# Where the taps of a convolution and the pieces of an output projection stand in the order of a two-layer hybrid trunk

## The chip, the core and the metric

The kernel runs on one core of one Trainium2 chip. The metric is the device time of one execution in microseconds; the time given for a kernel is the median of its runs. Traces come from one profiled execution. Engines are named as in the profile: PE is TensorE, DVE VectorE, ACT ScalarE, POOL GpSimd, SP SyncE.

## What is computed

Two decoder layers over 512 tokens of width 1024, in float32. Of each layer the part that matters here is its first half:

```python
n = rmsnorm(h, mix_norm[i])
u = n @ w_in[i]                                   # 1024 -> 9 x 256 columns
a_val, a_gate, pool_in, q, k, v, gb, gc, sv = jnp.split(u, IN_SPLITS, axis=-1)
y_a = conformer_conv(a_val, a_gate, ...)          # glu, causal depthwise conv of 31 taps, layernorm, silu
y_b = pool_mixer(pool_in, ...)                    # causal window means of 2, 4, 8, 16
y_c = diff_attention(q, k, v, ...)                # 4 heads x 2 maps, rotary, softmax(a0) - lam * softmax(a1)
y_d = short_gated_conv(gb, gc, sv, ...)           # 3 taps
h = h + jnp.concatenate([y_a, y_b, y_c, y_d], -1) @ w_out[i]
```

After it come a mixture of sixteen experts (top 2 of one group of four), a gated embedding projection, and at the end of the second layer a norm.

## The kernel before

Matrix products that must be exact to float32 are done as three products of split operands: each value is a high part and a low part (`wh`/`wl` for weights, `nhi`/`nlo`, `mhi`/`mlo` for activations), and `mm3` (L255 to L257) multiplies high by high, high by low and low by high. ScalarE makes the high half of a weight tile (L228), VectorE the low half (L239); `w.get` makes them three half units ahead of their use, and SP's queue loads the raw tiles four units ahead.

*The projection* (`project`, L431) goes through units of 256 columns; a half unit is 24 matmuls of 512 columns. After each half unit `tick` (L157) is called with a budget, `BUDGET`, less the cost of other VectorE work of that half unit. It first issues what is due, then takes entries from a queue while any budget is left:

```python
for c, fn in self.due.pop(self.t, []):
    fn()
    budget -= c
while self.queue and budget > 0:
    c, fn = self.queue.pop(0)
    fn()
    budget -= c
```

In the queue stand the 31 taps of the long convolution for each of two halves of the channels, 62 a layer, each an instruction on VectorE over 512 tokens (L480 for the first, L483 for the others), entered at a cost of 0.6; behind them stands the layer norm (`layer_norm`, L646). That is a cost in the planner's own units, not a time. GpSimd sums the pooling windows meanwhile (L513).

*Attention* (`attend`, L693) has 16 steps, one for a head and a block of 128 queries, and each engine's work of one step follows the list `TICK` (L53): transposes of q and k (L721), row maxima of the step before (L770), additions of finished pieces to the residual h (L750), attention times values (L816), exponentials (L784), the piece `f1`, the transpose of the combined probabilities (L804, copied by ScalarE at L806), what is due, the scores (L762), the piece `f2`, the combination of the two maps (L795 to L797). `due` goes on with the queue of taps, with budgets of its own (`TAPS`, L54); when the taps are used up, layer norm enters it and spreads its stages over the next steps: transposes (L656), statistics (L658, L661), a reciprocal root on GpSimd (L204, L205), normalising (L666), transposes back (L671), scale and tanh on ScalarE (L673, L675), the product (L678), and the split into `mhi` (L682) and `mlo` (L686).

The output projection of a block of 128 tokens, a half of its columns and a half of its rows is two *pieces*, each of six matmuls (L255 to L257 with `mhi`, `mlo`). The first 16 pieces read the pooling and short convolution outputs and can run from the start; three are issued before the first step, thirteen are dealt out by the tables `FILL1` (the piece or pieces at `f1` of step n) and `FILL2` (at `f2`). The others need layer norm and attention and start at step 11 (`WO1`); an entry that asks for more pieces than there are gets what is left:

```python
while k > 0 and (cur or (fill and fill[0][0] <= n)):
    ...
"f1": lambda n: filler(2 * n, FILL1[n]),
"f2": lambda n: filler(2 * n + 1, FILL2[n]),
```

A piece pair accumulates in one PSUM bank and keeps it until its addition to h. In attention eight banks are split into four for scores and pieces, three for transposes, one for the attention output.

Of the kernel before, what the change touches and what calls it, by code (L numbers as in the profile page):

```python
# [40 lines left out]
NCON, NCON2, NCON3 = 322, 256, 512  # L41
NOIDX = 2048.0
PAD_L, PAD_R, PAD_M = 224, 224, 160
BUDGET = 3.1
NRING, NRING2, NRING3, NRING4 = 4, 3, 4, 2
WO1 = 22
FILL1 = [0, 1, 1, 1, 1, 1, 0, 5, 1, 1, 1, 1, 1, 4, 0, 1, 0, 2, 1, 1, 0, 0, 0, 0, 0, 0, 0, 0, 0]
FILL2 = [4, 0, 1, 0, 0, 1, 0, 4, 1, 0, 0, 1, 0, 0, 0, 1, 2, 1, 2, 1, 2, 2, 4, 2, 2, 2, 0, 0, 0]
WARM0, WARM, PRE = 17, 11, 7
TAILU, POST, FIRST, FIRST4 = 9, 3, 5, 1  # L50
HI = {5: 1, 6: 2, 9: 3, 10: 4}
# [116 lines left out]
class _Kernel:  # L168
# [255 lines left out]
    def cm_unit(self, between=None, cost=0.0):  # L424
        o = [self.mm([128, S]) for _ in range(2)]
        for hf in range(2):
            self.cm_half(o, self.w.get(between=between if hf == 0 else None), hf)
            self.ticks.tick(BUDGET - cost if hf == 0 else BUDGET)
        return o

    def project(self):  # L431
# [154 lines left out]
        for hf in range(2):  # L586
            hi, lo = (t.rearrange("p (c n) -> p c n", c=4) for t in w.get(between=ev_gb if hf == 0 else None))
            for i in range(NT):
                ts = slice(i * 128, (i + 1) * 128)
                for c in range(4):  # L590
                    k = 4 * hf + c
                    self.mm3(o_v[i], self.nhi[:, k, ts], self.nlo[:, k, ts], hi[:, c], lo[:, c], k == 0, k == 7)
            tk.tick(BUDGET - (2.4 if hf == 0 else 0))
        pb_.close_()
# [10 lines left out]
        def qk(i, half, k0):  # L605
            ts = slice(i * 128, (i + 1) * 128)
            hi, lo = (t.rearrange("p (c n) -> p c n", c=2) for t in half)
            for c in range(2):
                k = k0 + c
                self.mm3(o[i], self.nhi[:, k, ts], self.nlo[:, k, ts], hi[:, c], lo[:, c], k == 0, k == 7)  # L610
# [3 lines left out]
        for hf in range(2):  # L614
            if hf:
                half = w.get()
            for i in range(NT):
                qk(i, half, 2 * hf)
            tk.tick(BUDGET)
        hv = [w.get(1), w.get(1)]  # L620
# [72 lines left out]
    def attend(self):  # L693
# [201 lines left out]
        def filler(n, k):  # L895

            while k > 0 and (cur or (fill and fill[0][0] <= n)):
                if not cur:
                    a = fill.pop(0)[1]
                    cur.append((a, wo_mm(*a)))  # L900
                    next(cur[0][1])
                else:
                    (i, nh, kh), g = cur.pop()
                    next(g)
                    if (nh, kh) == (1, 1) and i < 2:
                        for d, f in zip(FND, (fn1, fn3, fn2, fn4, fn5)):
                            tk.later(d, lambda f=f, i=i: f(i))
                k -= 1
# [35 lines left out]
        def each(table, f):  # L944
# [20 lines left out]
            "hi": lambda n: n in HI and w.make_hi(base + HI[n]),  # L965
            "f1": lambda n: filler(2 * n, FILL1[n]),
            "f2": lambda n: filler(2 * n + 1, FILL2[n]),
        }
# [608 lines left out]
```

## Time and profile before

| | |
|---|---|
| median of 3 runs | 923.5 us (921.14 to 924.35) |
| profiled execution | 922.49 us, span 920.7 us |
| projection, first layer | about 20 to 122 us of the span |
| attention steps, first layer | 130 to 200 us |
| projection, second layer | about 470 to 571 us |
| attention steps, second layer | 580 to 650 us |

The span is what lies between the first and the last instruction of the trace; 1.8 us of the execution lie around it. In a row of the timeline the first number is the start in us from the span's start, the second the length of the run of instructions that the row merges (their count is at its end), and in square brackets stands how long the engine was idle before and what it waited for. An instruction's length in the trace overlaps the next one's start a little, so a run of n is shorter than n times the mean length.

### The profile page before, as it was taken

Reading aid. Unit: us, or ns where it says so; the run is one execution under the profiler, and the core shown is the slowest. Engines: PE = TensorE matmul, PEld = TensorE weight load, DVE = VectorE, ACT = ScalarE, POOL = GpSimd, SP = SyncE. Lnnn points to the kernel's source line nnn. Section 1 sums busy time; section 2 is a strip of 40 time slices with the busy share of each in tenths; the row PEclk is TensorE's granted clock in tenths of the full one; section 3 lists DMA queues with packets and bytes.
Section 4 is the critical chain, followed back from the end, with each engine's and each line's share of the span. In section 5 each row is a group of like instructions: output and inputs, shape, how many; then the busy total and the mean of one; then the engine's idle time right before and its main releaser. Section 6 shows DMA issues by size and latency. Waiting matters only on the chain. (4 is left out here: it accounts for less than half of the span.)

```text
span 920.7 us, 12343 instructions
## 1 busy us (share of the span) xinstructions
PE 852.5 (93%) x4393; PEld 684.7 (74%) x4393; DVE 707.4 (77%) x1182; ACT 515.4 (56%) x929; POOL 155.2 (17%) x214
## 2 busy tenths in 40 slices
PE   6999999897999999989979999989969999998894
PEld 5888877785677777667878887767847777776783
DVE  4499979966788888746676987998478888885674
ACT  4322236853687877745433232487437778776453
POOL 2050001122222211101010400022131222111101
PEclk8999999998999999999999999999979999999998
DMA  9322330158799979663322233110968998882602
GB/s 346 116 92 92 103 114 1 47 195 308 266 347 363 370 272 340 236 221 160 115 92 92 92 103 115 46 47 29 386 219 296 373 370 311 315 320 94 258 24 91
DMA packets 35775, 179.02 MB, mean 194 GB/s; under 512 B 8064, under 2 KB 8320, under 8 KB 18944
## 3 DMA queue, kind: packets, MB, share of 16 engines
q1 hardware_dynamic: 23472, 148.49, 43.1%
q0 software_dynamic: 9792, 20.99, 6.2%
q10 hardware_dynamic: 2448, 8.73, 2.7%
q8 instruction: 35, 0.57, 0.3%
q14 instruction: 28, 0.23, 0.1%
HBM read 171.89 MB, written 23.07 MB: 212 GB/s over the span
## 5 line engine op out<-in xcount | busy, mean ns | idle before, releaser
L239 DVE TENSOR_TENSOR wl<-wr,wh 128x1024 fp32r<-128x1024 f32 x212 | 255.1, 1230 | 44.4 <-ACT wh L228 43.2
L228 ACT CAST wh<-wr 128x1024 fp32r<-128x1024 f32 x212 | 216.2, 1053 | 92.6 <-PE mm L256 61.0
L255 PE MATMUL mm<-wh,xTh 128*128 128x512 f32 x256 | 114.5, 447 | 0.7 <-ACT xTh L221 0.7
L257 PE MATMUL mm<-wh,xTl 128*128 128x512 f32 x256 | 101.3, 396 | 1.2 <-DVE xTl L222 1.2
L256 PE MATMUL mm<-wl,xTh 128*128 128x512 f32 x256 | 100.8, 394 | 0.0
L483 DVE SCALAR_TENSOR_TENSOR acc<-glu,cwh,acc 128x512 f32<-128x512 f32 x120 | 90.5, 819 | 0.1
L257 PE MATMUL mm<-nhi,wl 128*128 128x512 f32 (+1 forms) x224 | 77.3, 345 | 2.5 <-DVE wl L239 2.5
L255 PE MATMUL mm<-nhi,wh 128*128 128x512 f32 (+1 forms) x224 | 77.1, 344 | 0.0
L256 PE MATMUL mm<-nlo,wh 128*128 128x512 f32 (+1 forms) x224 | 77.0, 344 | 0.0
L255 PEld LDWEIGHTS mm<-wh,xTh 128*128 128x128 f32 x256 | 48.4, 189 | 16.6 <-issue 6.7
L1198 POOL DMA_INDIRECT xg<-xnd,ix x32 | 34.9, 1091 | 151.1 <-PE tr L251 137.9
L1241 PE MATMUL mm<-wr,hT 128*128 128x512 f32 x128 | 60.2, 592 | 0.0
L256 PEld LDWEIGHTS mm<-wl,xTh 128*128 128x128 f32 x256 | 48.5, 190 | 15.4 <-DVE wl L239 6.2
L257 PEld LDWEIGHTS mm<-wh,xTl 128*128 128x128 f32 x256 | 48.2, 188 | 12.8 <-DVE xTl L222 2.7
L255 PE MATMUL mm<-wh,mhi 128*128 128x512 f32 x128 | 54.1, 422 | 0.4 <-DVE h L750 0.4
L1203 POOL DMA_INDIRECT yd<-ys,ix x32 | 32.3, 1011 | 122.9 <-ACT ys L1243 107.3
L255 PE MATMUL mm<-wh,n3h 128*128 128x512 f32 x128 | 50.5, 395 | 0.0
L257 PE MATMUL mm<-wh,mlo 128*128 128x512 f32 x128 | 50.3, 393 | 0.0
L256 PE MATMUL mm<-wl,mhi 128*128 128x512 f32 x128 | 50.0, 390 | 0.0
L257 PE MATMUL mm<-wh,n3l 128*128 128x512 f32 x128 | 49.9, 390 | 0.0
L256 PE MATMUL mm<-wl,n3h 128*128 128x512 f32 x128 | 49.9, 390 | 0.0
L221 ACT CAST xTh<-tr 128x512 fp32r<-128x512 f32 x64 | 34.5, 590 | 25.2 <-PE tr L251 23.7
(235 smaller groups left out, 1860.6 us busy)
## 6 DMA issues: line engine op xcount, KB each, us to landing
wr<-wgu SPq DMA_DIRECT2D x62, 1024.0 KB, 9.2
wr<-wdn SPq DMA_DIRECT2D x30, 1024.0 KB, 11.0
wr<-win SPq DMA_DIRECT2D x13, 1024.0 KB, 6.6
wr<-wout SPq DMA_DIRECT2D x8, 1024.0 KB, 4.8
wr<-wpg SPq DMA_DIRECT2D x8, 1024.0 KB, 14.2
yt<-yd SPq DMA_DIRECT2D x12, 512.0 KB, 8.5
wr<-wqk SPq DMA_DIRECT2D x4, 1024.0 KB, 4.7
xnd<-xn ACTq DMA_DIRECT2D x8, 512.0 KB, 6.5
```

Source lines behind the costliest of these rows:

```text
L221: self.SC.copy(hi, src)
L228: self.SC.copy(hi, src)
L239: self.V.tensor_sub(lo, src, h32)
L255: self.T.matmul(o, lh, rh, start=first, stop=False)
L256: self.T.matmul(o, lh, rl, start=False, stop=False)
L257: self.T.matmul(o, ll, rh, start=False, stop=last)
L483: V.scalar_tensor_tensor(acc[:, m], glu[:, m, k:k + S], self.cwh[:, m, k:k + 1], acc[:, m], op0=ALU.mult, op1=ALU.add)
L1198: return self.G.indirect_dma_start(out=dst, out_offset=None, in_=self.xnd[:, :], in_offset=bass.IndirectOffsetOnAxis(ap=col, axis=0), boun ...
L1203: return self.G.indirect_dma_start(out=self.yd[:, :], out_offset=bass.IndirectOffsetOnAxis(ap=col, axis=0), in_=src, in_offset=None, bound ...
L1241: self.T.matmul(o[nh], hT[:, c], wc[:, ns], start=(c == 0), stop=(c == 1))
```

## The change

The budget of a half unit in the projection goes from 3.1 to 3.7, and the two tables deal the thirteen pieces out differently: of before there were four at `f2` of step 0 and up to five asked for at `f1` of step 7 (two were left); now two stand at `f2` of step 0, and one at `f1` of each step up to step 9.

```diff
-BUDGET = 3.1
+BUDGET = 3.7
-FILL1 = [0, 1, 1, 1, 1, 1, 0, 5, 1, 1, 1, 1, 1, 4, 0, 1, 0, 2, 1, 1, 0, 0, 0, 0, 0, 0, 0, 0, 0]
-FILL2 = [4, 0, 1, 0, 0, 1, 0, 4, 1, 0, 0, 1, 0, 0, 0, 1, 2, 1, 2, 1, 2, 2, 4, 2, 2, 2, 0, 0, 0]
+FILL1 = [0, 1, 1, 1, 1, 1, 1, 1, 1, 1, 1, 1, 1, 4, 0, 1, 0, 2, 1, 1, 0, 0, 0, 0, 0, 0, 0, 0, 0]
+FILL2 = [2, 0, 1, 0, 0, 1, 0, 0, 0, 0, 0, 1, 0, 0, 0, 1, 2, 1, 2, 1, 2, 2, 4, 2, 2, 2, 0, 0, 0]
```

The instructions of SP's queue stay in the same order. On VectorE the taps in the projection change as follows (`acc<-glu,cwh,acc` is a tap, `wl<-wr,wh` the low half of a weight tile), from the first half units of the first layer; first before:

```order
L480 TENSOR_SCALAR acc<-glu,cwh,par 128x512 x2
L483 SCALAR_TENSOR_TENSOR acc<-glu,cwh,acc 128x512 x2
L239 TENSOR_TENSOR wl<-wr,wh 128x1024
L483 SCALAR_TENSOR_TENSOR acc<-glu,cwh,acc 128x512 x6
L239 TENSOR_TENSOR wl<-wr,wh 128x1024
L483 SCALAR_TENSOR_TENSOR acc<-glu,cwh,acc 128x512 x6
L239 TENSOR_TENSOR wl<-wr,wh 128x1024
```

And the same place now:

```order
L480 TENSOR_SCALAR acc<-glu,cwh,par 128x512 x2
L483 SCALAR_TENSOR_TENSOR acc<-glu,cwh,acc 128x512 x3
L239 TENSOR_TENSOR wl<-wr,wh 128x1024
L483 SCALAR_TENSOR_TENSOR acc<-glu,cwh,acc 128x512 x7
L239 TENSOR_TENSOR wl<-wr,wh 128x1024
L483 SCALAR_TENSOR_TENSOR acc<-glu,cwh,acc 128x512 x7
L239 TENSOR_TENSOR wl<-wr,wh 128x1024
```

One tap more stands in every half unit that has any; a layer has eleven such places, so 61 taps stand in the projection and not 50.

VectorE in the second and third step of the first layer's attention (`mx` row maxima, `h` an addition of a finished piece, `fac` and `e` the combination of the two maps), before:

```order
L770 TENSOR_REDUCE mx<-mm 128x1 x2
L750 TENSOR_TENSOR h_113<-h_113,mm 128x512
L750 TENSOR_TENSOR h_114<-h_114,mm 128x512
L713 TENSOR_TENSOR qks<-qr_968,qks 128x8x32
L483 SCALAR_TENSOR_TENSOR acc<-glu,cwh,acc 128x512 x4
L795 RECIPROCAL fac<-sums 128x1
L796 SCALAR_TENSOR_TENSOR fac<-fac,nlam,sums 128x1
L797 SCALAR_TENSOR_TENSOR e_1274<-e_1276,fac,e_1274 128x128
L770 TENSOR_REDUCE mx<-mm 128x1 x2
L750 TENSOR_TENSOR h_115<-h_115,mm 128x512
L483 SCALAR_TENSOR_TENSOR acc<-glu,cwh,acc 128x512 x4
```

And now (`bst`, `bmv` are layer norm's statistics):

```order
L770 TENSOR_REDUCE mx<-mm 128x1 x2
L750 TENSOR_TENSOR h_113<-h_113,mm 128x512
L713 TENSOR_TENSOR qks<-qr_977,qks 128x8x32
L658 BN_STATS bst<-tr 128x6
L661 BN_AGGR bmv<-bst 128x2
L795 RECIPROCAL fac<-sums 128x1
L796 SCALAR_TENSOR_TENSOR fac<-fac,nlam,sums 128x1
L797 SCALAR_TENSOR_TENSOR e_1268<-e_1270,fac,e_1268 128x128
L770 TENSOR_REDUCE mx<-mm 128x1 x2
L750 TENSOR_TENSOR h_114<-h_114,mm 128x512
L666 TENSOR_SCALAR acc<-acc,bmv,lr 128x2x128
```

The eight taps are gone from these steps, one addition has moved a step down, and layer norm begins in the second step, three steps sooner.

TensorE in the ninth step of the first layer's attention, up to its scores (`tr<-con,qks` transposes of q or k, `oacc` attention times values, `tr<-con,e` the transpose of the probabilities, `tr<-con,acc` those of layer norm), before:

```order
L721 MATMUL tr<-con,qks 96x128 x4
L816 MATMUL oacc<-v_961,at 128x64
L816 MATMUL oacc<-v_962,at 128x64
L804 MATMUL tr<-con,e_1582 128x128 x2
L671 MATMUL tr<-con,acc 128x128 x2
L656 MATMUL tr<-con,acc 128x128 x2
L845 MATMUL tr<-con,on 128x128 x2
L762 MATMUL mm<-KT,QT 128x384
```

And now:

```order
L816 MATMUL oacc<-v_970,at 128x64
L816 MATMUL oacc<-v_971,at 128x64
L255 MATMUL mm<-wh,mhi 128x512
L256 MATMUL mm<-wl,mhi 128x512
L257 MATMUL mm<-wh,mlo 128x512
L255 MATMUL mm<-wh,mhi 128x512
L256 MATMUL mm<-wl,mhi 128x512
L257 MATMUL mm<-wh,mlo 128x512
L804 MATMUL tr<-con,e_1609 128x128 x2
L845 MATMUL tr<-con,on 128x128 x2
L762 MATMUL mm<-KT,QT 128x384
```

A piece stands now between the attention output and the transpose, and layer norm's transposes have gone to earlier steps.

## Rows read from the trace of the kernel before

**Rows 1.** The page, busy us of the engines.

```profile
PE 852.5 (93%) x4393; PEld 684.7 (74%) x4393; DVE 707.4 (77%) x1182; ACT 515.4 (56%) x929; POOL 155.2 (17%) x214
```

**Rows 2.** Busy time by stage: stretch and length, engines, granted clock, DMA share, GB/s.

```profile
500.00:570.00 70.00, 70.00 (x352) 59.29 (x351) 63.93 (x92) 19.51 (x27) 12.84 (x12) 1.00 0.24 82
...
579.60:626.00 46.40, 40.42 (x242) 31.84 (x240) 43.96 (x120) 32.59 (x95) 7.59 (x14) 1.00 0.13 46
590.00:600.00 10.00, 9.53 (x59) 7.65 (x58) 9.35 (x30) 5.73 (x20) 0.62 (x2) 1.00 0.01 2
611.00:626.00 15.00, 11.26 (x81) 8.81 (x78) 13.70 (x36) 14.51 (x42) 3.07 (x5) 1.00 0.21 71
```

**Rows 3.** VectorE's timeline in the second layer's projection, up to attention.

```profile
498.94 1.23 DVE L239 TENSOR_TENSOR wl<-wr,wh 128x1024 fp32r<-128x1024 f32 x1 [1.12 <-ACT wh L228]
...
504.38 1.23 DVE L239 TENSOR_TENSOR wl<-wr,wh 128x1024 fp32r<-128x1024 f32 x1 [0.24 <-ACT wh L228]
505.52 6.49 DVE L483 SCALAR_TENSOR_TENSOR acc<-glu,cwh,acc 128x512 f32<-128x512 f32 x6
...
513.94 5.90 DVE L483 SCALAR_TENSOR_TENSOR acc<-glu,cwh,acc 128x512 f32<-128x512 f32 x6
...
538.54 0.69 DVE L222 TENSOR_TENSOR mlo<-sA,mhi 128x512 fp32r<-128x512 f32 x1 [1.21 <-ACT mhi L221]
539.87 0.69 DVE L222 TENSOR_TENSOR mlo<-sA,mhi 128x512 fp32r<-128x512 f32 x1 [0.64 <-ACT mhi L221]
...
560.22 4.07 DVE L483 SCALAR_TENSOR_TENSOR acc<-glu,cwh,acc 128x512 f32<-128x512 f32 x6
...
572.36 0.94 DVE L713 TENSOR_TENSOR qks<-qr,qks 128x256 fp32r<-128x256 f32 x2 [4.44 <-ACT qks L708]
```

**Rows 4.** GpSimd's timeline there: the first and the last of six window sums.

```profile
504.91 1.62 POOL L513 TENSOR_TENSOR sA<-up 128x527 f32<-128x527 f32 x1 [30.27 <-ACT up L504]
...
507.08 1.58 POOL L513 TENSOR_TENSOR sB<-sA 64x526 f32<-64x526 f32 x1
...
516.16 1.81 POOL L513 TENSOR_TENSOR sB<-sA 64x520 f32<-64x520 f32 x1
```

**Rows 5.** TensorE's timeline at the entry into the second layer's attention.

```profile
572.85 1.96 PE L721 MATMUL tr<-con,qks 128*96 128x128 f32 x16 [1.71 <-DVE qks L713]
```

**Rows 6.** What TensorE waited for, 579.6 to 626: us, times, longest.

```profile
PE oacc L816 <- ACT at L806: 2.0, 2, 1.3
PE tr L721 <- ACT at L806: 1.0, 1, 1.0
PE tr L804 <- DVE e L797: 0.8, 4, 0.3
PE tr L845 <- ACT at L806: 0.7, 1, 0.7
PE mm L762 <- ACT e L784: 0.6, 2, 0.3
```

**Rows 7.** What ScalarE waited for, 579.6 to 626.

```profile
ACT e L784 <- DVE mx L770: 3.5, 3, 1.4
```

**Rows 8.** TensorE's timeline: the first scores, one of two pieces, the eighth, ninth, twelfth scores.

```profile
579.68 0.36 PE L762 MATMUL mm<-KT,QT 96*128 96x256 f32 x1
...
608.27 0.48 PE L255 MATMUL mm<-wh,mhi 128*128 128x512 f32 x1
...
611.09 0.38 PE L804 MATMUL tr<-con,e 128*128 128x128 f32 x2
...
611.44 0.36 PE L762 MATMUL mm<-KT,QT 96*128 96x256 f32 x1
...
615.75 0.42 PE L762 MATMUL mm<-KT,QT 96*128 96x384 f32 x1
...
625.85 0.42 PE L762 MATMUL mm<-KT,QT 96*128 96x384 f32 x1
```

**Rows 9.** VectorE's timeline: the first of three groups of taps in attention.

```profile
579.75 2.73 DVE L483 SCALAR_TENSOR_TENSOR acc<-glu,cwh,acc 128x512 f32<-128x512 f32 x4
```

## The prediction

> **What bounds the kernel now.** I read the page's first section, then busy time by stage, then VectorE's timeline through the second layer's projection and attention, then who waits for whom in attention. Over the span TensorE is busy 93% and VectorE 77% [rows 1], but that average hides two different stages. In the projection TensorE is busy 70.00 of 70.00 us while VectorE has 63.93 [rows 2]: TensorE alone sets the time there, and nothing it waits for is late. From the first scores of attention to the twelfth (the 46.4 us of the second row of that group) TensorE is busy 40.42, so it stands idle 5.98, and VectorE is busy 43.96, the fuller of the two. The third and fourth rows split this: from 590 to 600 TensorE idles 0.47 in 10 us; from 611 to 626 it idles 3.74 in 15, VectorE has 13.70 and ScalarE 14.51. So the early steps are packed with projection pieces on TensorE and the late ones wait. For whom is in [rows 6]: the largest rows name ScalarE's copy of the turned probabilities (L806), 2.0, 1.0 and 0.7 us; only 0.8 names VectorE. But ScalarE itself waited 3.5 us for VectorE's row maxima (L770) [rows 7], so part of what is booked on ScalarE comes from a late VectorE. The first layer shows the same steps; all numbers below are from the second, whose clock was 1.00 in these rows.
>
> **The change, part by part.** Two things move, nothing is added: of the 62 taps of a layer 50 ran in the projection and 12 in attention (three groups of four); now 61 and 1 do. And of the thirteen pieces of the output projection that run up to the tenth step, two leave the stretch after the first scores and one the stretch after the seventh; one each goes to the stretches after the sixth, eighth and ninth.
>
> *Taps in the projection.* A tap costs 4.07/6 = 0.68 us (the row at 560.22 of [rows 3]). I follow VectorE's lateness through its waits. The first extra tap falls before a wait of 1.12 us and vanishes in it. The second meets 0.24: 0.44 late. Five more come before the next wait: 0.44 + 5 x 0.68 = 3.84 late. There two waits of 1.21 and 0.64 for ScalarE give 1.85 back: 1.99 late. The last four: 4.71 late at the end of the taps. Then VectorE sits idle 4.44 us before the first L713 (the row at 572.36 of [rows 3]), so 0.27 is left, and since TensorE waits for just that instruction with 1.71 us already [rows 5], I charge 0.3 us a layer. Before that point nothing shows: VectorE makes the low halves of the weights (L239) three half units before TensorE reads them, and one half unit is 504.38 - 498.94 = 5.44 us, so 4.7 us late is under the 16.3 of the cover. The loads on SP's queue that wait for these halves keep their order and stand four units ahead. If the 4.44 us were not there, all 4.71 would fall on TensorE.
>
> What is least sure is the tap's price where GpSimd works. From 504.91 to 517.97 its window sums run [rows 4], and the two groups of six taps in that stretch took 6.49 and 5.90 us, up to 1.08 each instead of 0.68 (the rows at 505.52 and 513.94 of [rows 3]). VectorE has no gap there already, so an extra tap does not lengthen GpSimd's work: it is pushed behind it, and I price it at 0.68. The other end is 1.08 for every one of the eleven: 11.9 us, less the cover of 0.68 + 0.24 + 1.85 + 4.44 = 7.21, is 4.7 us late a layer. There is no end below nothing: the instructions only grow in number.
>
> That the two engines are in each other's way is also in the Trainium skill (SBUF — State Buffer, "Who interferes with whom"): a VectorE instruction with two inputs in SBUF and a GpSimd one that reads SBUF exclude each other for the whole instruction. By that rule a tap could wait for a whole sum of 1.58 us [rows 4]; for the three extra taps of that stretch that is 4.7 us more, about the far end just given and a slower kernel. The trace agrees that they collide, not with that size: 0.40 us a tap.
>
> *Attention.* Taken out of VectorE: 11 x 0.68 = 7.5 us of 43.96, leaving 36.5; TensorE's work stays 40.4. Two bounds follow. If every wait of TensorE goes, a layer gains 5.98; if the softmax chain and not VectorE's load is what it waits for, nothing (or what [rows 6] books on VectorE, 0.8). A gain above 5.98 is excluded, since TensorE has no less to do; a loss here needs a new wait, see below. The pieces move at no cost of their own: one is (611.09 - 608.27)/2 = 1.41 us [rows 8], the stretch from 611.44 to 615.75 has no piece today and holds waits, and what the others gain the first and seventh give back.
>
> For the middle I use the two rows of [rows 2]. Up to 611 the stretch is 46.4 - 15 = 31.4 us with 5.98 - 3.74 = 2.24 us of waits. With one piece a step and VectorE at 93% the row from 590 to 600 idles 0.047 of its time, so 1.5 us stay. From 611 on there were no taps to take away (the last of the three groups of four that begin at 579.75 [rows 9] ends before 593) and VectorE is still busy 13.70 of 15 us, so what helps there is indirect: layer norm starts three steps earlier, so its VectorE and ScalarE work leaves this stretch, and pieces fill waits. I let half of the 3.74 stay, 1.9. So 1.5 + 1.9 = 3.4 stay and 2.6 us a layer go. What layer norm moves with it (transposes, ScalarE copies and activations, two short GpSimd instructions a block) lands in steps 1 to 5, where ScalarE has 5.73 of 10 us and GpSimd 0.62 [rows 2].
>
> New waits: a piece that is split over two steps keeps one of four PSUM banks while the next scores need two, so scores can wait for the exponentials that free the last pair. Today that is 0.6 us in two waits, 0.3 each [rows 6]. Bounds: nothing, or 0.3 in each of five steps, 1.5; I count it inside the 3.4 that stay.
>
> *Sum.* (2.6 - 0.3) x 2 layers = 4.6 us. The profiled execution took 922.49, span 920.7 and 1.8 around it: 922.49 - 4.6 = 917.9. The median shown, 923.5, is 1.0 above the profiled one: **918.9**.
>
> **Rivals.**
> *All waits go* (for it: work sums put TensorE alone on top, 40.4 against 36.5; against: the late stretch had no taps and still idles). (5.98 - 0.3) x 2 = 11.4: 912.1.
> *The chain sets the steps, not the load.* Scores, maxima, exponentials, combination, transpose, copy follow one another across engines; for it: the large rows of [rows 6] name ScalarE, which is busy 14.51 of 15 in that stretch. Then only the 0.8 booked on VectorE goes: (0.8 - 0.3) x 2 = 1.0: 922.5, no change.
> *VectorE enters attention late.* Place: the first L713 after the projection. Price: the far end of the taps, 4.7 us a layer, for it the 1.08 us of the taps beside GpSimd, against it that most extra taps run where GpSimd is idle. It makes the kernel slower from the point at which L713 comes more than 2.6 us later than now; at 4.7: (4.7 - 2.6) x 2 = 4.2 more: 927.7.
> That the change would not do what it says is excluded for the counts by the order of the instructions.
>
> **How the numbers follow.** About 0.3%, 2.8 us, is what a measurement of this kernel can tell from no change, so faster means under 920.7 and slower above 926.3. Forecast 0.52 (its own range 915 to 921), all waits 0.06, chain 0.28, late VectorE 0.14. Faster: 0.49 of the forecast, 0.06, and 0.05 of the chain case, where a little more goes: 0.60. Same: the remaining 0.03 and 0.23: 0.26. Slower 0.14. The range from 914 to 925 leaves out the all-waits case and the late VectorE, 0.20.
>
> **What would show it.** After: a tap group of one and not of four at the first step; VectorE's wait before the first L713 of attention shrunk from 4.44 to under 0.5 us, TensorE's wait there 1.7 to 2.2; no wait of TensorE in the projection; twelfth scores 2.6 us sooner after the first ones; TensorE's waits in that stretch 3.4 us and not 6. Wrong if L713 is over 1 us late, if the waits of [rows 6] on L806 stay whole (chain), or if attention gains and the mixture of experts behind it does not start as much earlier.

## The result, and the profile after

The changed kernel takes 911.65 us (median of 7 runs, 910.83 to 916.55) where the kernel before, beside it, took 922.54 (919.62 to 924.35): ratio 0.9895, 95% interval 0.9873 to 0.9917. The profiled execution took 910.88, its span 909.1, against 922.49 and 920.7. So the change is worth about 11 us where 4.6 were forecast: the sign was right, the size was not, and the time lies under the range.

The page of after, busy us of the engines ([rows 1]). TensorE's instructions are as many and its total is nearly what it was, so the 11.6 us of span are not work that went away:

```profile
PE 851.7 (94%) x4393; PEld 684.5 (75%) x4393; DVE 706.6 (78%) x1182; ACT 515.0 (57%) x929; POOL 157.6 (17%) x214
```

Busy time by stage in the second layer of after ([rows 2]; the same stages, 5.5 us sooner at the first scores): the projection, attention from the first scores to the twelfth, and from that stretch its early and its late part. Columns are stretch, length, PE, PEld, DVE, ACT, POOL, granted clock, DMA share, GB/s:

```profile
495.00:565.00 70.00, 70.00 (x352) 59.27 (x351) 68.12 (x99) 19.54 (x27) 13.12 (x12) 1.00 0.23 79
574.10:615.60 41.50, 39.24 (x243) 31.86 (x240) 37.18 (x111) 32.89 (x96) 8.24 (x14) 1.00 0.15 52
584.50:594.50 10.00, 9.68 (x61) 7.68 (x60) 9.44 (x33) 8.57 (x29) 0.95 (x2) 1.00 0.01 2
600.60:615.60 15.00, 13.70 (x90) 11.01 (x88) 14.10 (x36) 13.10 (x37) 2.96 (x4) 1.00 0.20 71
```

TensorE is still busy 70.00 of 70.00 us in the projection, though VectorE now has 68.12. Attention is where the time went: from the start of the first scores to that of the twelfth it is 615.58 - 574.20 = 41.38 us, against 46.17 in [rows 8], and 41.38 against 46.21 in the first layer. That is 9.6 of the 11.6 us. The last 15 us of the stretch idle 1.30 and not 3.74. The remaining 2 us are not put down to the change: the first scores of the two layers come 0.3 us sooner each, 0.4 gather between the twelfth scores of the second layer and the experts behind it, and 0.9 come at the head of these experts, behind a wait for a DMA. There the granted clock was 0.60 in the 4.3 us from the first transposes (L251) on in before, and 1.00 in after; the transposes, before and after:

```profile
682.70 1.77 PE L251 MATMUL tr<-con,xg 128*128 128x128 f32 x8 [1.91 <-DMA xg<-xnd,ix]
672.06 1.09 PE L251 MATMUL tr<-con,xg 128*128 128x128 f32 x8 [1.71 <-DMA xg<-xnd,ix]
```

VectorE's timeline of after in the projection and at the door of attention (its first transposes), seven taps to a group ([rows 3]):

```profile
500.37 7.96 DVE L483 SCALAR_TENSOR_TENSOR acc<-glu,cwh,acc 128x512 f32<-128x512 f32 x7
508.25 1.21 DVE L239 TENSOR_TENSOR wl<-wr,wh 128x1024 fp32r<-128x1024 f32 x1
509.39 6.57 DVE L483 SCALAR_TENSOR_TENSOR acc<-glu,cwh,acc 128x512 f32<-128x512 f32 x7
515.88 1.22 DVE L239 TENSOR_TENSOR wl<-wr,wh 128x1024 fp32r<-128x1024 f32 x1
...
566.87 0.94 DVE L713 TENSOR_TENSOR qks<-qr,qks 128x256 fp32r<-128x256 f32 x2 [0.21 <-ACT qks L708]
```

And TensorE's of after: the door ([rows 5]), the first and the twelfth scores ([rows 8]):

```profile
567.36 1.95 PE L721 MATMUL tr<-con,qks 128*96 128x128 f32 x16 [1.71 <-DVE qks L713]
...
574.20 0.36 PE L762 MATMUL mm<-KT,QT 96*128 96x256 f32 x1
...
615.58 0.42 PE L762 MATMUL mm<-KT,QT 96*128 96x384 f32 x1
```

VectorE's 4.44 us of idle time ahead of L713 are down to 0.21, and TensorE waits there the same 1.71 as before. What TensorE waits for in attention, 574.1 to 615.7 (us in total, times, longest; [rows 6]):

```profile
PE mm L762 <- DVE h L750: 0.7, 1, 0.7
PE mm L762 <- ACT e L784: 0.6, 1, 0.6
PE tr L804 <- DVE e L797: 0.4, 2, 0.2
PE tr L721 <- DVE qks L713: 0.4, 1, 0.4
PE oacc L816 <- ACT at L806: 0.3, 1, 0.3
```

The waits for the copy L806, 3.7 us in three rows before, are one of 0.3. The fourth row lies ahead of the first scores. ScalarE's wait for the row maxima in the same stretch ([rows 7]) has halved:

```profile
ACT e L784 <- DVE mx L770: 1.8, 4, 0.9
```

### The profile page after: what moved, and what is told of

Read it like the earlier page. It is cut to its first block, busy times and chain, and to the rows that moved or that the text cites. A ratio compares the mean times of both kernels' runs of the same rounds, so it can differ in the third digit from the quotient of the medians.

```text
span 909.1 us, 12343 instructions
## 1 busy us (share of the span) xinstructions
PE 851.7 (94%) x4393; PEld 684.5 (75%) x4393; DVE 706.6 (78%) x1182; ACT 515.0 (57%) x929; POOL 157.6 (17%) x214
## 5 line engine op out<-in xcount | busy, mean ns | idle before, releaser
L239 DVE TENSOR_TENSOR wl<-wr,wh 128x1024 fp32r<-128x1024 f32 x212 | 253.2, 1221 | 42.0 <-ACT wh L228 40.5
L483 DVE SCALAR_TENSOR_TENSOR acc<-glu,cwh,acc 128x512 f32<-128x512 f32 x120 | 91.7, 830 | 0.1
L257 PEld LDWEIGHTS mm<-nhi,wl 128*128 128x128 f32 x224 | 42.4, 189 | 8.1 <-DVE wl L239 3.2
```

The lines of the kernel that those rows point to most:

```text
L239: self.V.tensor_sub(lo, src, h32)
L257: self.T.matmul(o, ll, rh, start=False, stop=last)
L483: V.scalar_tensor_tensor(acc[:, m], glu[:, m, k:k + S], self.cwh[:, m, k:k + 1], acc[:, m], op0=ALU.mult, op1=ALU.add)
```

## The experiments

All ratios are to the kernel before on the same chip, with 95% intervals. To compare steps, the start of the first matmul of each step's scores (L762) is taken from TensorE's timeline and the differences are summed: "early" is first to sixth scores, "late" sixth to twelfth. The stretch holds the same 14 pieces in every kernel; the old tables put 10 into the early part and 4 into the late one, the new tables 8 and 6.

| kernel | taps in attention | tables | layer norm | early | late | sum |
|---|---|---|---|---|---|---|
| before | 12 | old | late | 22.40 | 23.77 | 46.17 |
| no_att_taps | 0 | old | late | 20.81 | 23.84 | 44.65 |
| budget_only | 1 | old | early | 21.87 | 22.44 | 44.31 |
| tables_only | 12 | new | late | 21.79 | 24.60 | 46.39 |
| late_norm | 1 | new | late | 18.09 | 24.59 | 42.68 |
| after | 1 | new | early | 19.15 | 22.23 | 41.38 |

(budget_only and tables_only from the first layer, whose granted clock was 1.00 over the whole stretch; the others from the second, at 1.00 too.)

### One half of the change at a time: budget_only and tables_only

```diff
-BUDGET = 3.1
+BUDGET = 3.7
```

> Only the taps move (budget 3.7), the pieces stand as before. The span from the first to the twelfth scores of a layer (46.2 us before, 41.4 after) tells. If VectorE's load is what the late steps waited for, most of the gain is here: 43 us, so about 6 us of the 10.9 in all, and the waits for ScalarE's copy L806 shrink, while the stretches after the eighth to tenth scores, which have no piece, keep some 2 us of waits for the softmax chain. If the pieces' places are what fills the waits, it stays at 45.5 us and the time within 2 us of before.

919.16 us, ratio 0.9949 (0.9923 to 0.9975). The 44.31 us from first to twelfth scores lie between the two expectations. The second layer took 45.87: there the clock fell in one of the late steps (last section), and this is part of the time of 919.16. The waits for L806 stay whole without the new tables; what TensorE waits for in the second layer's steps of budget_only:

```profile
PE oacc L816 <- ACT at L806: 3.4, 3, 1.6
PE mm L762 <- ACT e L784: 0.7, 1, 0.7
```

The other half is the new FILL1 and FILL2 with the old budget.

> Only the pieces move, the taps stand as before (12 in attention). If VectorE's load decides: VectorE had 1.3 us of gaps in 46.2, so it can't be done sooner; first to twelfth scores 45 to 46.2 us, time as before within 2 us, with TensorE's waits now in the first three steps where the taps stand and two pieces less cover them. If the places of the pieces decide: 43 us and some 6 us less in all.

924.9 us, ratio 1.0032 (1.0009 to 1.0055): a little slower, with 46.39 us from first to twelfth scores where 45 to 46.2 or 43 were expected. With four taps a step still on VectorE, the pieces taken out of the first steps uncover a wait there, for VectorE's combination of the two maps; in the second layer of tables_only:

```profile
PE tr L804 <- DVE e L797: 2.0, 3, 1.1
PE oacc L816 <- ACT at L806: 0.8, 1, 0.8
PE tr L845 <- ACT at L806: 0.7, 1, 0.7
```

Alone the halves give -0.5% and +0.3%, together -1.05%. In the steps of the table, all at a clock of 1.00, they give 46.17 - 44.31 = 1.86 us and a loss of 0.22, together 4.79. The gain is not a sum of two.

### The load alone: no_att_taps

The kernel before, without the twelve taps a layer that stand in attention; that part of the convolution is left out.

```diff
-                    tk.queue.append((0.6, tap(m, k)))
+                    tk.queue.append((0.6, tap(m, k) if 2 * k + m < 50 else lambda: None))
```

> The kernel before without the 12 taps of attention (they are left out of the convolution, in both layers); layer norm and pieces stand in the steps of before, the projection is untouched. If VectorE's load decides: first to twelfth scores about 43 us as with the budget alone, since 8.2 us of VectorE's work are gone. If layer norm's earlier start decides: over 45 us. If the places of the pieces decide: over 45.5 us.

919.02 us, ratio 0.9964 (0.9947 to 0.9982), with 44.65 us from first to twelfth scores where 43 were expected if VectorE's load decides. All of the gain, 1.59 us a layer, is won in the early steps. The late waits are those of the kernel before; rows of no_att_taps that answer to [rows 6]:

```profile
PE oacc L816 <- ACT at L806: 2.0, 2, 1.3
PE tr L721 <- ACT at L806: 1.0, 1, 1.0
PE tr L845 <- ACT at L806: 0.7, 1, 0.7
```

So VectorE's load did not make the late waits. And TensorE is busy less although it does the same (stretch of no_att_taps, columns as above; 242 instructions, 40.19 us busy in the same stretch of before):

```profile
578.95:623.60 44.65, 39.34 (x242) 31.56 (x239) 36.14 (x108) 32.49 (x94) 7.61 (x14) 1.00 0.13 48
```

### Layer norm's start alone: late_norm

The kernel after, with every stage of layer norm three steps later, where it was before.

```diff
-                tk.later(d + LNT[i], lambda f=f, i=i: f(i))
+                tk.later(d + LNT[i] + 3, lambda f=f, i=i: f(i))
```

> The changed kernel, but layer norm's stages are put three steps later, to the steps in which they stood before; taps and pieces as changed. If the load that the taps took from VectorE is what counts, wherever layer norm stands: first to twelfth scores 41.4 to 42.2 us and the time of the changed kernel within 1.5 us. If layer norm's earlier start, which takes ScalarE's and VectorE's work out of the late steps, gave the second half of the gain: 43.5 us or more, some 4 us slower than the changed kernel.

916.17 us, ratio 0.9932 (0.9903 to 0.9962), 42.68 us from first to twelfth scores in both layers, between the two expectations. The moved pieces alone have cut the waits for L806 from 3.7 us (no_att_taps) to 1.5; rows of the second layer of late_norm:

```profile
PE oacc L816 <- ACT at L806: 0.8, 1, 0.8
PE tr L845 <- ACT at L806: 0.7, 1, 0.7
```

Against it the kernel after pays 19.15 - 18.09 = 1.06 us in the early steps and wins 24.59 - 22.23 = 2.36 in the late ones: layer norm's earlier start is worth 1.30 a layer with the new tables. With the old ones (no_att_taps against budget_only) it costs the same 1.06 and wins 1.40: 0.34 (budget_only has one tap in attention that no_att_taps lacks).

The table then gives a way from before to after in three steps (the second also brings back the one tap that no_att_taps lacks, and another order would share out the sum otherwise): taps out, 46.17 - 44.65 = 1.52; pieces moved, 44.65 - 42.68 = 1.97; layer norm earlier, 1.30. The sum is 4.79. The same pieces moved with the taps still there (before to tables_only) lose 0.2.

### The price of the taps in the projection: no_extra_taps

The kernel after, without the eleven taps a layer that the change put into the projection; part of the convolution is left out.

```diff
-                    tk.queue.append((0.6, tap(m, k)))
+                    tk.queue.append((0.6, (lambda: None) if 2 * k + m in out_ else tap(m, k)))
```

> The kernel after without the eleven convolution taps a layer that the change put into the projection (part of the convolution is left out), so that their price shows: attention has no tap, as in the kernel after, and the layer norm starts where it does there. Theory A, the prediction's price: TensorE runs through the projection without a wait, and the taps cost 0.3 us a layer there at most, so 911.0 to 911.7 us (0.9993 to 1 of the kernel after), with the wait for the first transposes of attention near 1.7 us as in the kernel after. Theory B, the far end of the range: each tap makes VectorE late for attention; then some us a layer come back, 905 to 908.

911.3 us, ratio 0.9867 (0.9837 to 0.9898), which can't be told from the kernel after; a price of 0.6 us in all could hide in these intervals. The traces are finer. The door of no_extra_taps shows the wait that it shows with the taps:

```profile
568.04 1.96 PE L722 MATMUL tr<-con,qks 128*96 128x128 f32 x16 [1.71 <-DVE qks L714]
```

From the first transposes of the second layer's projection (L251) to its last matmul it takes 94.56 us, 94.55 in the kernel after and 94.56 in the kernel before, and the steps of attention agree too (41.34 and 41.38). In the traces the price is nothing, not 0.3 us.

### A VectorE that does come late: more_taps

The kernel after, with four more taps a layer behind the projection's last matmuls (they are counted twice).

```diff
+        for k in (1, 2):
+            for m in range(2):
+                tap(m, k)()
```

> The kernel after with four more taps a layer (two channels, taps one and two again, so the convolution counts them twice), put on VectorE right behind the last matmuls of the projection and ahead of the rotation of the first tile, where nothing can hide them: 4 x 0.675 = 2.7 us of VectorE. It measures what a late VectorE costs at the door of attention. Theory A: the first transposes wait for VectorE, and all of it is lost: the wait of the first transposes goes from 1.7 to about 4.3 us, 2.6 us a layer, 916.9 us. Theory B: the room that attention has since the change (no tap there) takes part of it back in the first steps: the stretch from the first transposes to the twelfth scores gets 1 to 2 us shorter, 913 to 915.

920.35 us, ratio 0.9963 (0.9944 to 0.9983): 8.7 us more than the kernel after by the medians, which come from two sets of runs (the kernel before at 922.54 and at 923.99), 6.3 by the ratios and 9.0 by the spans, where 5.2 were the worst expectation. The door and the clock beside it, second layer of more_taps:

```profile
574.54 0.88 PE L724 MATMUL tr<-con,qks 128*96 128x128 f32 x3 [4.18 <-DVE qks L716]
```

The stretches from that wait on (columns as above, the granted clock third from the end):

```profile
570.40:574.50 4.10, 0.00 (x0) 0.00 (x0) 4.00 (x12) 1.82 (x3) 0.00 (x0) 0.89 0.41 128
574.50:580.00 5.50, 5.46 (x21) 4.94 (x22) 2.95 (x10) 3.52 (x6) 0.00 (x0) 0.50 0.53 192
580.00:582.00 2.00, 2.00 (x9) 1.59 (x9) 2.00 (x2) 1.22 (x2) 0.00 (x0) 0.89 0.00 0
```

The wait grew by 4.18 - 1.71 = 2.47 us, as the taps' length says. But behind it the granted clock is 0.50, which is the lower of TensorE's two levels, 1.2 and not 2.4 GHz, and from the first transposes to the first scores it takes 9.07 us and not 6.84 (7.90 in the first layer). Door and clock make (2.47 + 2.23) + (2.44 + 1.06) = 8.2 of the 9.0 us between the two spans. The steps of attention stay at 41.35 and 41.40: nothing is won back there. So a late VectorE would have been dearer than my rival had it; it was not late.

### One piece half a step sooner: piece_sooner

In the kernel after the largest wait left, 0.72 us, is scores that wait for an addition to free a bank. Here the piece ahead of the tenth scores stands behind the ninth.

```diff
-FILL1 = [0, 1, 1, 1, 1, 1, 1, 1, 1, 1, ...
-FILL2 = [2, 0, 1, 0, 0, 1, 0, 0, 0, 0, ...
+FILL1 = [0, 1, 1, 1, 1, 1, 1, 1, 1, 0, ...
+FILL2 = [2, 0, 1, 0, 0, 1, 0, 0, 1, 0, ...
```

> The kernel after with the last early output piece one half step sooner (behind the scores of the ninth step and not ahead of those of the tenth), so that its addition is due a step sooner. In the kernel after TensorE waits 0.72 us in the eleventh step for that addition to free a bank (matmul of line 762 on VectorE's addition). Theory A: that wait goes and nothing comes for it: 0.7 us a layer, 910.2 us, first to twelfth scores 40.7. Theory B: where the piece was it covered the chain; the tenth step's transposes or its line 816 wait instead, as in the kernel before: 911.5 to 913, first to twelfth scores 41.4 or more.

912.61 us, ratio 0.9884 (0.9854 to 0.9914); 42.05 us from first to twelfth scores, 0.67 a layer more than in the kernel after. The wait for the addition has gone, but between the same two scores, the eleventh and the twelfth, the wait for L806 has grown from 0.3 to 1.3 us and taken it back. The loss stands one step sooner, where the tenth scores now wait for exponentials too (L784). Theory B had the time right and the place not: it named the tenth step's transposes or its L816. All waits of TensorE in these steps of piece_sooner:

```profile
PE oacc L816 <- ACT at L806: 1.3, 1, 1.3
PE mm L762 <- ACT e L784: 1.0, 2, 0.7
PE tr L804 <- DVE e L797: 0.4, 2, 0.2
```

### The wait that was left at the door: early_entry and early_entry2

The 1.71 us at the door are order as well: ScalarE stacks the first tile's queries only behind its copy of the last tile, and VectorE takes their low part behind the next weight part. Both are moved ahead (`...` stands for the definitions of `stack0` and `stack0_lo`, ScalarE's stack and VectorE's low part of the first tile, and at the end for the lines that take up what they made):

```diff
-        for b in range(2):
-            rotate(0, b)
-        for i in range(1, NT):
...
+        rotate(0, 0)
+        for i in (1, 2):
             SC.copy(qr[i].rearrange("p a d -> p (a d)"), o[i])
+        stack0(0)
+        rotate(0, 1)
+        stack0_lo(0)
+        stack0(1)
+        SC.copy(qr[3].rearrange("p a d -> p (a d)"), o[3])
+        stack0_lo(1)
         w.make_lo()
...
```

> The kernel after, with the first tile's stacked operands made earlier: the query half is stacked and its low part taken while the projection's last matmuls run, and ScalarE's copy of the last tile and VectorE's next weight part come behind them; the same instructions in another order. Theory A: what is left of the wait at the door of attention, 1.71 us, is only this order; it falls to some 0.3 us, 1.3 us a layer, 909.0 us, and the steps of attention keep their lengths. Theory B: the weight part that is now later makes the first output piece wait, or the steps' chain takes it back: the sum from the last matmul of the projection to the twelfth scores stays, 911 to 912.

912.66 us, ratio 0.9882 (0.9852 to 0.9913), which by itself can't be told from the kernel after. The trace can: in the second layer of early_entry the wait is 0.27, and the next one, for the second tile, has grown from 0.35 to 0.93:

```profile
567.06 1.96 PE L735 MATMUL tr<-con,qks 128*96 128x128 f32 x16 [0.27 <-DVE qks L645]
...
574.09 0.64 PE L735 MATMUL tr<-con,qks 128*96 128x128 f32 x4 [0.93 <-DVE qks L727]
```

From the last matmul of the projection to the first scores it takes 8.09 us and not 8.94: 0.85 us a layer where theory A expected 1.3. So the second tile's stack is put ahead of the next weight parts too:

```diff
-        wo_get(0, 1)
         stack(1, 0)
         stack_lo(1, 0)
+        wo_get(0, 1)
```

> The kernel with the earlier first stack (early_entry), and the second tile's query half also stacked sooner: its stack and low part stand ahead of the next two weight parts on ScalarE and VectorE and not behind them; the same instructions in another order. In early_entry the wait of the first transposes fell from 1.71 to 0.27 us, but the second tile's transposes then waited 0.93 and not 0.35, so from the start of the projection's last matmul to the first scores it took 8.09 us against 8.94 in the kernel after. Theory A: that second wait is order too: 8.09 falls to about 7.2, first to twelfth scores stay 41.4, 3.5 us below the kernel after. Theory B: the weight parts that are pushed back come too late for the next output piece, TensorE waits in its matmuls behind the first scores, and the first step gets longer by what was won: last projection matmul to twelfth scores as in early_entry, 49.5 us.

> The kernel after, unchanged, on the same chip as early_entry2, so that the two stand beside each other: last projection matmul to first scores 8.94 us, first to twelfth scores 41.4 us in both layers, ratio to the kernel before 0.9895 as measured first.

909.93 us, ratio 0.9842 (0.9819 to 0.9864), and the kernel after beside it 912.96, ratio 0.9888 (0.9865 to 0.991): 3.0 us, the two intervals just apart. The door of early_entry2, with the first scores:

```profile
568.60 1.95 PE L735 MATMUL tr<-con,qks 128*96 128x128 f32 x16 [0.28 <-DVE qks L645]
...
574.54 0.60 PE L735 MATMUL tr<-con,qks 128*96 128x128 f32 x4
574.90 0.36 PE L776 MATMUL mm<-KT,QT 96*128 96x256 f32 x1
```

The second wait is gone; from the last projection matmul to the first scores it takes 6.96 us (7.29 in the first layer) against 8.94 in the kernel after in both, 3.6 us in all, and the steps keep their 41.4. This version beats both kernels.

## Why the prediction was wrong

**The step that failed** is "I let half of the 3.74 stay, 1.9. So 1.5 + 1.9 = 3.4 stay and 2.6 us a layer go". Measured: of the late 3.74 us 1.30 stay, of the whole stretch's 5.98 stay 41.38 - 39.12 = 2.26, and 4.8 us a layer go. Two terms in it were mis-sized, about equally: of the 2.2 us a layer that are missing, 3.4 - 2.26 = 1.14 are waits that went beyond the forecast, and 1.07 come from TensorE's busy time. (In the two profiled executions 7.0 us are missing: 4.4 are these, 0.6 the charge for the door below, and 2.0 lie outside the change.)

*The pieces as cover* (work that TensorE can do where it would wait). The prediction moved them "at no cost of their own", what some stretches gain "the first and seventh give back", and then let them fill half of the late waits by a guess. The runs show an exchange that is not neutral: two pieces out of the early steps shorten these by 2.72 us (20.81 to 18.09) and lengthen the late ones by only 0.75 (23.84 to 24.59), since there they stand where TensorE waited for L806. But this holds only while the early steps can do without them. With the taps still on VectorE the same exchange gains 0.61 early and loses 0.83 late. That the one edit makes room for the other was in my text as a sum of separate terms, so it could not show.

*The idle time as a ceiling.* I wrote that "a gain above 5.98 is excluded, since TensorE has no less to do", and held its busy time at 40.4. Between the two scores it was 40.19 in the second layer and fell to 39.12 for the same 242 instructions, by 1.07 us, and in no_att_taps, where nothing but VectorE's load changed, already by 0.85. Busy time is not work here. Three rows of one piece in after:

```profile
607.47 0.40 PE L257 MATMUL mm<-wh,mlo 128*128 128x512 f32 x1
607.71 0.40 PE L255 MATMUL mm<-wh,mhi 128*128 128x512 f32 x1
607.94 0.39 PE L256 MATMUL mm<-wl,mhi 128*128 128x512 f32 x1
```

Each is 0.40 long and the next starts 0.23 later, so a matmul that comes up to 0.17 late leaves no gap in the busy time, and of a longer wait the first 0.17 count as busy. In no_att_taps, whose matmuls stand in the order of before, most of the 0.85 can be placed: three matmuls for which before lists waits of 0.19, 0.17 and 0.30 us start 0.57, 0.56 and 0.60 us after the one ahead of them there, and 0.23, 0.23 and 0.03 us after it in no_att_taps. That is 0.60 us of lost time that was listed as busy, beside 0.65 listed as idle. For the whole change the orders differ, and that its 1.07 are of the same kind is my reading.

**The taps in the projection.** The mechanism was right: no wait of TensorE in the projection, VectorE's wait at the door under the 0.5 us named, TensorE's wait 1.71 of the 1.7 to 2.2 named. The charge of 0.3 us a layer was too much: VectorE came out 4.44 - 0.21 = 4.23 us late at the door and not 4.71, inside the cover of 4.44, and no_extra_taps finds no price. Nor did the taps beside GpSimd reach the far end. The two groups of six of 6.49 and 5.90 us became groups of seven of 7.96 and 6.57, but the weight part between them (L239) took 1.21 and not 2.08. From the first group to the weight part behind the second it is 515.88 - 500.37 = 15.51 us and was 519.76 - 505.52 = 14.24, so the two added taps cost 1.27 together, 0.64 each, and the price of 0.68 held. Single instructions of that stretch in before:

```profile
507.66 1.55 DVE L483 SCALAR_TENSOR_TENSOR acc<-glu,cwh,acc 128x512 f32<-128x512 f32 x1
509.14 0.74 DVE L483 SCALAR_TENSOR_TENSOR acc<-glu,cwh,acc 128x512 f32<-128x512 f32 x1
...
511.94 2.08 DVE L239 TENSOR_TENSOR wl<-wr,wh 128x1024 fp32r<-128x1024 f32 x1
...
519.76 1.21 DVE L239 TENSOR_TENSOR wl<-wr,wh 128x1024 fp32r<-128x1024 f32 x1
```

The first tap starts inside the sum of 507.08 in [rows 4] and ends 0.55 us behind it; the second starts just ahead of the next sum and is as long as a tap alone. Beside each of the six sums one VectorE instruction is 0.8 to 1.1 us longer than alone: five taps and a weight part in before, six taps in after. So 1.08 was a mean of short taps and long ones, and a tap that is added while the sums stay six costs its own length. My working from the rule of the Trainium skill (SBUF — State Buffer, "Who interferes with whom") charged three added taps a whole sum each, 4.7 us; only two fall into that stretch, and they cost 1.27 together. The rule, that the one engine waits for the other, is in keeping with these rows; it was the number of meetings that I had wrong.

**Layer norm's start** was named, and its direction was right: it pays 1.06 early and wins 2.36 late. It had no number of its own in the sum.

**The rivals.** *All waits go* (912.1) came nearest in time, and for another reason than its own: 2.26 us of waits are left, and 1.07 of what went was not in the waits. *The chain sets the steps* is half true, and that half is what I under-used: no_att_taps shows that the late waits do not answer to VectorE's load at all. What closes them is work put into them (3.7 us of waits for L806 become 1.5 in late_norm) and layer norm's earlier start (0.3 in the kernel after). *VectorE enters late* did not happen; more_taps shows that it would have cost more than my price, by the clock.

**What I said would show it.** A group of one tap at the first step: yes (one L483 at 574.26, 0.75 us). Door: yes. Twelfth scores 2.6 us sooner: 4.8. Waits 3.4: 2.3. The experts start earlier by as much as attention gains: yes.

## What to carry to other kernels

Before pricing two edits as a sum, ask whether one makes room for the other: cover (independent matmuls) is worth its full length only where an engine waits, and it can be taken away only where nothing waits without it. Where pipelined instructions are listed longer than the distance between their starts, idle time is a lower bound of what a stretch can gain, not an upper one. And behind a gain, look at the door of the stage: an engine's order there (a copy or a weight part ahead of the instruction that everybody waits for) was worth 3 us here with no work changed.

## What the runs showed of the hardware

A long wait of TensorE was paid twice in more_taps. After 4.18 us without a matmul the granted clock was at 0.50 for the next 5.5 us, and 2.23 us were lost behind the wait; after the 1.71 us of the kernel after it stayed at 1.00. A wait between the two went both ways in budget_only: the same wait for L806 of 1.6 us, in the first layer without a loss,

```profile
158.59 0.66 PE L816 MATMUL oacc<-v,at 128*128 128x64 f32 x4 [1.63 <-ACT at L806]
```

and in the second with a clock of 0.70 behind it (matmuls 0.43 us apart and not 0.23), which made that step 8.48 us long and not 6.89:

```profile
604.00:607.00 3.00, 1.11 (x9) 0.70 (x7) 2.84 (x8) 2.97 (x10) 0.51 (x1) 1.00 0.00 0
607.00:610.00 3.00, 3.00 (x12) 2.48 (x13) 2.93 (x9) 2.60 (x7) 1.44 (x1) 0.70 0.00 0
```

TensorE's work was the same in both layers: busy 1.11 of the 3 us around the wait and 6.90 of the 7 us before, in the first as in the second. So neither the length of the wait nor the work around it tells the two apart; what does was not tried.
